# Gates of a product-key expert layer: element-wise adds into a zeroed DRAM array in place of one-hot matrices, on one Trainium2 core

## The chip, the core and the metric

The kernel runs on one core of a Trainium2 chip. The metric is the device time of one execution in microseconds (us); before the change the median of 3 runs is 3128.93 us (3125.25 to 3133.51). A core has TensorE (PE, its weight loads PEld), VectorE (DVE), ScalarE (ACT), GpSimd (POOL) and SyncE (SP); DMAs are issued by SP, ACT and POOL. L12 is line 12 of a kernel; lines of the kernel before and of the changed one differ, and the texts name the kernel where it isn't plain.

## What is computed

512 tokens of 1024 channels and 16 meta tokens pass through two layers. Each has a mixer (pooling in layer 0, stick-breaking attention in layer 1) and then an expert layer, PEER, with 128x128 = 16384 experts. PEER is what the change is about (q, the two halves of the keys and the experts u, v are inputs):

```python
s = einsum('bthpc,hpnc->bthpn', q, sub_keys)              # 8 heads, 2 halves, 128 keys
top_s, top_i = top_k(s, 16)
cand_s = top_s[..., 0, :, None] + top_s[..., 1, None, :]  # 256 candidates
cand_i = top_i[..., 0, :, None] * 128 + top_i[..., 1, None, :]
best_s, best_pos = top_k(cand_s, 16)
expert = take_along_axis(cand_i, best_pos)
gate = softmax(best_s)
act = gelu(einsum('btd,bthkd->bthk', h, u[expert]))
y = einsum('bthk,bthkd->btd', gate * act, v[expert])
```

A token thus has 8 heads x 16 slots = 128 pairs of an expert and a gate. The same expert can come up in several heads, and then its gates add; within one head the 16 experts are distinct.

## The kernel before

Tokens lie in four tiles of 128. Both layers run `peer` (L255). **Tile 3 is gathered** (`GATHERED`): for each of its 128 pairs an indirect DMA from POOL (L343, `row`) fetches one expert's u and v for each of the 128 tokens, 128 rows of 8 KB, and DVE forms the dot product (L355, `prod`) and adds the weighted v (L367, `hx`). Layer 0's meta tokens do the same with 16 more. These gathers are called rows below; `row_step` (L372) issues them a piece at a time, paced by `ROW_PERIOD`, in four buffers (`NROW`).

**Tiles 0 to 2 (384 tokens) are dense:** every block j of 128 experts is computed for every token, whether chosen or not. A u step (L307, matmuls L314) multiplies u of block j with the 384 tokens: fp32 is made of a high and a low part, so each product is three matmuls, 24 of 128x384 in a step, with ACT splitting off the high part (`w_hi`, L279) and DVE or POOL the low part (`w_lo`, L281 and L283). Its gelu, `ac`, goes to DRAM (`aout`). A v step (L660, matmuls L690) reads it back, multiplies it with the block's gates (`wt`, zero where the expert is not chosen) and adds wt times v into six PSUM banks y: 18 matmuls of 128x512.

So the gates have to be spread from 128 pairs to one number for each of 16384 experts and 384 tokens, 25 MB (`gout` in DRAM). Before the change `build_gates` (L553) does it in blocks of four tokens: DVE builds fp16 one-hot matrices of the two key indices by comparing with `iota_x` and multiplies the gate in, as a high and a low fp16 part (L593 to L596); PE multiplies two 128x128 matrices for each token and part (L574, L576, 8 matmuls in a block, 768 in a layer); ACT copies the result to `stage` (L581) and a DMA of 2 MB writes 32 tokens. The v step loads gates of four blocks j as `gt`, in pieces of 512 bytes.

A layer's PEER has three stages. In the **top-16 stage** each head's query is projected (L507, L508 in layer 0, L123 to L125 in layer 1), scored against the keys (L521), and DVE finds the 16 best in each half for each tile (`top16`, L391: MAX8, FIND_INDEX8, MATCH_REPLACE8); for tile 3 `select` (L399) then finds the 16 best pairs and their gates, also by one-hot comparisons (L439, L442, L445). POOL makes the `w_lo` here. A written plan mixes u steps in by estimated costs (`WQ_DVE`, `WQ_PE`). In the **gates stage** `gate_stream` (L606) selects for one dense tile at a time over all heads and then builds its gates; costs yielded by it (`DVE_SLACK`) decide after how much of it a quarter of a u step or a row step follows, and the matmuls' order on PE is pinned to that. In the **v stage** v steps and the remaining u steps run; PE has little else.

Each engine takes its instructions in an order fixed at build time, and a DMA issued by an engine stands in that engine's order.

Of the kernel before, what the change touches and what calls it, by code (L numbers as in the profile page):

```python
# [8 lines left out]
F32 = mybir.dt.float32  # L9
F32R = mybir.dt.float32r  # L10
F16 = mybir.dt.float16
BF = mybir.dt.bfloat16  # L12
I32 = mybir.dt.int32
# [21 lines left out]
GSCALE = 32768.0  # L35
NCAND = 80
TB = 32
FRONT = 3
UPARTS = 4
TG = 4  # L40
GLAG = 2
DVE_SLACK = 1.08
# [15 lines left out]
def trunk_kernel(ctx: ExitStack, tc: tile.TileContext, x, meta, norm_mix, norm_ffn, pool_w, pool_scale,  # L58
# [12 lines left out]
    iota_x = const([P, P, TG], F16, "iota_x")  # L71
# [12 lines left out]
    sy.dma_start(hx[0], x[0, :P, :])  # L84

# [43 lines left out]
    def pool_mixer(gain, normed):  # L129
        with tc.tile_pool(name="pm", bufs=1, reuse_waits="tile") as s1, \  # L130
# [8 lines left out]
            v.tensor_copy(iota_x, iota_f.unsqueeze(2).to_broadcast([P, P, TG]))  # L139
# [101 lines left out]
            pre(0)  # L241
            fold()
            for i in range(1, NT):
                pre(i)
            mixed(NT, hm, None)
            mixed(0, hx[0], NT)
            mixed(1, hx[1], 0)
# [7 lines left out]
    def peer(layer, with_meta, gain, hn_nat, kp, up, finish):  # L255
        gathered = list(GATHERED)
        dense = [i for i in range(NT) if i not in gathered]
        nd = len(dense)
        c0 = dense[0] * P
        assert dense == list(range(dense[0], dense[0] + nd))  # L260
        ND = nd * P
        NB = ND // TB
        gout = dram.tile([P, NB, NK, TB], F32, name=f"gout{layer}")
# [4 lines left out]
        with ExitStack() as cl:  # L268
# [5 lines left out]
            def load_w(src):  # L274
# [12 lines left out]
            pinned = [False]  # L287
            gating = [False]

            def pin(x):  # L290
                return tc.keep_in_program_order(x) if pinned[0] else x

# [14 lines left out]
            def u_parts(j, spill, following=None):  # L307
# [3 lines left out]
                for k in range(KC):  # L311
                    for a, b, st, en in ((whi, hi, k == 0, False), (whi, lo, False, False),
                                         (wlo, hi, False, k == KC - 1)):
                        m = pin(pe.matmul(ps[:, :ND], a[:, k, :], b[:, k, c0:c0 + ND], start=st, stop=en))  # L314
# [11 lines left out]
            def u_step(j, spill, following=None):  # L326
                return drained(u_parts(j, spill, following))

# [8 lines left out]
            def row_steps():  # L337
                flight = []

                def fetch():  # L340
                    item = todo.pop(0)
                    row = gr.tile([P, 2 * D], F32, name="row", bufs=NROW)
                    gp.indirect_dma_start(out=row, out_offset=None, in_=peer_uv,  # L343
                                          in_offset=bass.IndirectOffsetOnAxis(ap=item[1], axis=0))
# [37 lines left out]
            with ExitStack() as c1:  # L382
                tp = c1.enter_context(tc.tile_pool(name="tp", bufs=1, reuse_waits="tile"))
                ps1 = c1.enter_context(tc.tile_pool(name="ps1", bufs=2, reuse_waits="tile", space=PSUM))
                tv = [tp.tile([P, H, 2, TK], F32, name=f"tv{i}") for i in range(NT)]
# [13 lines left out]
                def select(tmp, outp, tag, tvi, tii, nh, res):  # L399
# [3 lines left out]
                    def st(name, dt=F32):  # L403
                        return tmp.tile([P, H * TK], dt, name=name)[:, :ns]
# [648 lines left out]
```

## Time and profile before

| | |
|---|---|
| median of 3 runs | 3128.93 us (3125.25 to 3133.51) |
| profiled execution, its own time | 3127.99 us |
| its span, first to last instruction | 3126.3 us |
| mean granted TensorE clock (1 is 2.4 GHz) | 0.984 |
| busy: PE, DVE, ACT, POOL | 96%, 78%, 43%, 22% |
| DMA | 758.52 MB, mean 243 GB/s |
| PEER of layer 0: top-16, gates, v stage | 55 to 233, 233 to 641, 641 to 1399 us |
| attention | 1399 to 1794 us |
| PEER of layer 1 | 1794 to 1988, 1988 to 2382, 2382 to 3122 us |

Busy shares are time in instructions; since matmuls overlap, their modelled ends make PE look full where one simply follows another, so what one costs is the distance of starts. The chain of what ended last is followed back from the last instruction to what released each step. The table by stage gives busy times in each stretch, the clock and the DMA rate. The stages were bounded by the first and last u, pg and y matmuls of each layer.

### The profile page before, as it was taken

What the parts mean: (1) busy time and instruction counts of PE and PEld (TensorE: products, weight loads), DVE (VectorE), ACT (ScalarE), POOL (GpSimd) and SP (SyncE); (2) the same over time, 40 slices, a digit from 0 to 9 for tenths busy, and PEclk for the clock granted to TensorE, in tenths of its full rate; (3) what the DMA queues carried; (4) which work ended last, traced back from release to release, by engine and by line L of the source; (5) the groups of instructions that cost most, each with busy time, mean ns of one, the idle gap of its engine ahead of it and who ended that gap; (6) DMA issues with size and microseconds to landing.
All of it is one profiled execution on the core that took longest, in us unless ns stands there. A gap on an engine that the chain in (4) does not pass through costs nothing.

```text
span 3126.3 us, 45813 instructions
## 1 busy us (share of the span) xinstructions
PE 2999.0 (96%) x16514; PEld 2671.7 (85%) x16514; DVE 2449.1 (78%) x5636; ACT 1354.3 (43%) x2184; POOL 688.7 (22%) x704
## 2 busy tenths in 40 slices
PE   8988999999999999999999989799999999999999
PEld 7887988988888888879965778798898888888887
DVE  3999998878777778786456469999987777777765
ACT  3443645643333333335455334354655333333333
POOL 3431311111111111114245244222110111111100
PEclk9999999999999999999999999999999999999999
DMA  3435877799989899762100344477878998989875
GB/s 134 179 121 202 282 265 265 274 360 329 338 312 321 314 329 329 273 245 90 55 1 1 108 177 144 158 262 269 303 253 326 358 314 321 331 308 333 307 250 164
DMA packets 286708, 758.52 MB, mean 243 GB/s; under 512 B 23184, under 2 KB 176784, under 8 KB 248336
## 3 DMA queue, kind: packets, MB, share of 16 engines
q1 hardware_dynamic: 222544, 390.92, 36.8%
q0 software_dynamic: 39168, 285.23, 24.9%
q10 hardware_dynamic: 24768, 79.44, 6.6%
q8 instruction: 129, 2.11, 0.3%
q14 instruction: 99, 0.81, 0.1%
HBM read 673.99 MB, written 81.53 MB: 242 GB/s over the span
## 4 chain that ended last, share of the span: by engine, by line
PE 77%; DVE 16%; DMA 3%; ACT 2%; issue 1%; POOL 0%; SPq 0%; DVEq 0%; ACTq 0%; POOLq 0%
PE y L690 31%; PE psu L314 27%; PE pg L574 3%; PE pg L576 3%; PE pp L124 2%; PE pp L125 2%; PE pp L123 2%; DVE mr L395 1%; DVE prod L355 1%; DVE w_lo L281 1%; DMA gt<-gout 1%; DVE ti L397 1%; DVE hx L367 1%; DMA w<-in_peer_ut_dram 1%; DVE ti L394 1%
## 5 line engine op out<-in xcount | busy, mean ns | idle before, releaser
L343 POOL DMA_INDIRECT row<-in_peer_uv_dram,ei x272 | 383.3, 1409 | 1833.1 <-DVE hx L367 1481.9
L314 PE MATMUL psu<-n_hi,w_lo 128*128 128x384 f32 x2048 | 701.5, 343 | 42.4 <-DVE w_lo L281 39.9
L314 PE MATMUL psu<-n_hi,w_hi 128*128 128x384 f32 x2048 | 720.4, 352 | 11.5 <-ACT ac L321 7.2
L314 PE MATMUL psu<-n_lo,w_hi 128*128 128x384 f32 x2048 | 703.0, 343 | 0.6 <-DVE n_lo L118 0.6
L279 ACT ACTIVATE w_hi<-w 128x1024 fp32r<-128x1024 f32 x288 | 305.6, 1062 | 467.7 <-PE psu L314 373.2
L690 PE MATMUL y<-v_lo,wt_hi 128*128 128x512 f32 x1536 | 473.6, 390 | 1.6 <-DVE v_lo L676 1.6
L690 PE MATMUL y<-v_hi,wt_hi 128*128 128x512 f32 x1536 | 473.8, 390 | 0.5 <-ACT v_hi L675 0.5
L690 PE MATMUL y<-v_hi,wt_lo 128*128 128x512 f32 x1536 | 473.6, 389 | 0.0
L314 PEld LDWEIGHTS psu<-n_hi,w_lo 128*128 128x128 f32 x2048 | 394.0, 192 | 49.0 <-DVE w_lo L281 45.8
L314 PEld LDWEIGHTS psu<-n_hi,w_hi 128*128 128x128 f32 x2048 | 395.4, 193 | 17.8 <-ACT ac L321 7.5
L314 PEld LDWEIGHTS psu<-n_lo,w_hi 128*128 128x128 f32 x2048 | 394.0, 192 | 5.5 <-DVE n_lo L118 1.1
L682 ACT ACTIVATE wt_hi<-wt 128x384 fp32r<-128x384 f32 x256 | 134.3, 525 | 574.0 <-PE y L690 295.5
L683 DVE TENSOR_TENSOR wt_lo<-wt,wt_hi 128x384 fp32r<-128x384 f32 x256 | 142.5, 557 | 264.3 <-ACT wt_hi L682 264.3
L281 DVE TENSOR_TENSOR w_lo<-w,w_hi 128x1024 fp32r<-128x1024 f32 x228 | 278.2, 1221 | 83.2 <-ACT w_hi L279 82.6
L690 PEld LDWEIGHTS y<-v_lo,wt_hi 128*128 128x128 f32 x1536 | 288.1, 188 | 63.3 <-DVE v_lo L676 2.9
L690 PEld LDWEIGHTS y<-v_hi,wt_lo 128*128 128x128 f32 x1536 | 288.3, 188 | 60.4
L355 DVE SCALAR_TENSOR_TENSOR prod<-row,hnat 128x1024 bf16<-128x1024 f32 x272 | 337.7, 1241 | 0.6 <-DMA row<-in_peer_uv_dram,ei 0.5
L367 DVE SCALAR_TENSOR_TENSOR hx<-row,gwt,hx 128x1024 f32<-128x1024 f32 x256 | 334.5, 1307 | 2.1
L690 PEld LDWEIGHTS y<-v_hi,wt_hi 128*128 128x128 f32 x1536 | 286.8, 188 | 52.8 <-ACT v_hi L675 0.9
L676 DVE TENSOR_TENSOR v_lo<-v,v_hi 128x1024 fp32r<-128x1024 f32 x256 | 312.2, 1219 | 5.4 <-ACT v_hi L675 5.2
L581 ACT ACTIVATE stage<-pg 128x512 f32<-128x512 f32 x192 | 216.9, 1137 | 149.2 <-PE pg L576 146.3
L675 ACT ACTIVATE v_hi<-v 128x1024 fp32r<-128x1024 f32 x256 | 270.8, 1058 | 10.6 <-DMA v<-in_peer_uv_dram 9.5
(313 smaller groups left out, 4695.0 us busy)
## 6 DMA issues: line engine op xcount, KB each, us to landing
w<-in_peer_ut_dram SPq DMA_DIRECT2D x256, 512.0 KB, 5.9
v<-in_peer_uv_dram SPq DMA_DIRECT2D x256, 512.0 KB, 6.1
gout<-stage ACTq DMA_DIRECT2D x24, 2048.0 KB, 8.4
gt<-gout SPq DMA_DIRECT2D x64, 768.0 KB, 10.2
aout<-ac ACTq DMA_DIRECT2D x148, 192.0 KB, 4.0
ac<-aout SPq DMA_DIRECT2D x148, 192.0 KB, 5.9
w<-in_peer_wq_dram SPq DMA_DIRECT2D x32, 512.0 KB, 3.4
wn<-in_w_kv_dram SPq DMA_DIRECT2D x8, 1024.0 KB, 5.5
```

Source lines behind the costliest of these rows:

```text
L279: amark.append(sc.activation(whi, w, AF.Copy))
L281: vmark.append(v.tensor_sub(wlo, w, whi.bitcast(F32)))
L314: m = pin(pe.matmul(ps[:, :ND], a[:, k, :], b[:, k, c0:c0 + ND], start=st, stop=en))
L343: gp.indirect_dma_start(out=row, out_offset=None, in_=peer_uv, in_offset=bass.IndirectOffsetOnAxis(ap=item[1], axis=0))
L355: v.scalar_tensor_tensor(prod, row[:, :D], 1.0, hn_nat[i], ALU.mult, ALU.mult, accum_out=dot)
L367: v.scalar_tensor_tensor(acc, row[:, D:], wt, acc, ALU.mult, ALU.add)
L581: sc.activation(stage[:, :, o:o + TG].rearrange("p j t -> p t j"), pg, AF.Copy, scale=1.0 / GSCALE)
L675: amark.append(sc.activation(vhi, v32, AF.Copy))
L676: vmark.append(v.tensor_sub(vlo, v32, vhi.bitcast(F32)))
L682: sc.activation(whi, wt, AF.Copy)
L683: vmark.append(v.tensor_sub(wlo, wt, whi.bitcast(F32)))
L690: pe.matmul(y[n][half], wp[:, ts], vq[:, half * 512:(half + 1) * 512], start=st, stop=en)
```

## The change

The gates of the dense tiles are no longer built but added into place. `gout` is an array of 6,291,456 floats for each layer, laid out as key 1, key 2, token. It is zeroed ahead of time (`clear_gates`): in layer 0 by six DMAs of 4.2 MB that ACT issues during the pooling mixer, in layer 1 by four during the attention. In the top-16 stage `select` now runs once per head, over all four tiles (64 slots a token), and `gates_out` computes with two DVE operations an address `at` for each pair. `scatter` then issues, from POOL, one indirect DMA with an add for each head, tile and slot: 128 addresses, one for each partition, 4 bytes each. There are 8x3x16 = 384 in a layer; 27 are issued in each head's place in the program, the rest between the u steps that follow, up to the 122nd (`EARLY`). As adds of different heads may meet at one element, a head's scatters wait for those of the head before on the same tile. The gate matrices, their matmuls, stage copies and 2 MB writes go, and the gates stage with its pinned order: after the top-16 stage there are u steps, with row steps at a new `ROW_PERIOD`, then the v stage. All `w_lo` are made by DVE. `gt` becomes [128, 4, 384] with 6 KB in one run, and its load waits for the last head's scatters.

```diff
-ROW_PERIOD = ((18.0, 13.5), (18.0, 13.5))
-WQ_DVE = (19.0, 19.0)
-WQ_PE = (15.5, 12.5)
+ROW_PERIOD = (12.0, 13.0)
+WQ_DVE = 27.5
+WQ_PE = (15.5, 14.5)
-QUIET = 16
+EARLY = 122
+SCATTER_A = 27
...
+    gouts = [dram.tile([P * NK * ND, 1], F32, name=f"gout{layer}") for layer in range(2)]
+    cleared = [[], []]
+    def clear_gates(layer, part, parts):
+        g = gouts[layer].rearrange("(p c f) o -> p c (f o)", p=P, f=512)
+        n = NK * ND // 512 // parts
+        cleared[layer].append(sc.dma_start(g[:, part * n:(part + 1) * n, :],
+                                           zero.unsqueeze(1).to_broadcast([P, n, 512])))
...
-                if gating[0]:
-                    vmark.append(v.tensor_sub(wlo, w, whi.bitcast(F32)))
-                else:
-                    gp.tensor_sub(wlo, w, whi.bitcast(F32))
+                vmark.append(v.tensor_sub(wlo, w, whi.bitcast(F32)))
...
+            def gates_out(h, i1, i2, gate):
+                ef = gr.tile([P, nd, TK], F32, name="gf", bufs=2)
+                at = gr.tile([P, nd * TK], I32, name=f"at{h}")
+                ds = slice(0, nd * TK)
+                v.scalar_tensor_tensor(ef, i1[:, ds].rearrange("p (n q) -> p n q", q=TK), float(ND),
+                                       tok[:, :nd].unsqueeze(2).to_broadcast([P, nd, TK]), ALU.mult, ALU.add)
+                v.scalar_tensor_tensor(at, i2[:, ds], float(NK * ND), ef.rearrange("p n q -> p (n q)"),
+                                       ALU.mult, ALU.add)
+                to_scatter.extend((h, n, at[:, n * TK + q:n * TK + q + 1], gate[:, n * TK + q:n * TK + q + 1])
+                                  for n in range(nd) for q in range(TK))
+            def scatter(count):
+                for _ in range(min(count, len(to_scatter))):
+                    h, n, at, gate = to_scatter.pop(0)
+                    x = gp.indirect_dma_start(out=gout, out_offset=bass.IndirectOffsetOnAxis(ap=at, axis=0),
+                                              in_=gate, in_offset=None, compute_op=ALU.add)
+                    if issued:
+                        after(x, issued[0], sync=False)
+                    issued.append(x)
+                    earlier = placed[n, h - 1] if h else cleared[layer]
+                    for e in earlier:
+                        after(x, e)
...
                 def fetch():
...
+                    for y in issued:
+                        after(x, y, sync=False)
+                    issued[:] = [x]
...
+                        i1, i2, gate = select(qp, gr, f"h{h}", tv, ti, NT)
+                        gates_out(h, i1, i2, gate)
+                        scatter(SCATTER_A)
                         for i in gathered:
-                            res = []
-                            for _ in select(qp, gr, f"g{i}_{h}", tv[i][:, h:h + 1], ti[i][:, h:h + 1], 1, res):
-                                pass
-                            gather_rows(i, h, *res, TK, hx[i], False)
-                        while tr < tq and row_step():
-                            tr += ROW_PERIOD[layer][0] / 8
+                            of = slice(i * TK, (i + 1) * TK)
+                            gather_rows(i, h, i1[:, of], i2[:, of], gate[:, of], TK, hx[i], False)
...
+                left = len(to_scatter)
+                first = j0
                 tu = tr = 0.0
+                while j0 < EARLY:
+                    u_step(j0, True, ("u", j0 + 1))
+                    j0 += 1
+                    scatter(left * (j0 - first) // (EARLY - first) - (left - len(to_scatter)))
+                    tu += ucost
+                    while tr < tu and row_step():
+                        tr += ROW_PERIOD[layer] / 8
+                scatter(len(to_scatter))
...
+                        gts[jg] = vp.tile([P, JG, ND], F32, name="gt", bufs=3)
+                        x = sy.dma_start(gts[jg], gates[:, jg * JG:(jg + 1) * JG, :])
+                        for n in range(nd):
+                            for e in placed[n, H - 1]:
+                                after(x, e)
```

What the change does to the order, at the places that the prediction speaks of.

POOL in layer 0's top-16 stage, before (`row` is a gather of tile 3, `ei_0` the expert numbers of head 0, `w_lo` a low part; "x3" is three in a row):

```order
L283 TENSOR_TENSOR w_lo<-w_1183,w_hi 128x1024
L343 DMA row<-in_peer_uv_dram,ei_0_988 128x2048 x3
L283 TENSOR_TENSOR w_lo<-w_1217,w_hi 128x1024
L343 DMA row<-in_peer_uv_dram,ei_0_988 128x2048
L283 TENSOR_TENSOR w_lo<-w_1323,w_hi 128x1024
L343 DMA row<-in_peer_uv_dram,ei_0_988 128x2048
```

and with the change (`at_1008` are the addresses of head 0, `h0gate` its gates):

```order
L353 DMA gout_82<-h0gate,at_1008 6291456x1 x48
L353 DMA gout_82<-h1gate,at_1538 6291456x1 x48
L353 DMA gout_82<-h2gate,at_1932 6291456x1 x48
L353 DMA gout_82<-h3gate,at_2326 6291456x1 x48
L353 DMA gout_82<-h4gate,at_2720 6291456x1 x25
L380 DMA row<-in_peer_uv_dram,ei_0_1040 128x2048 x3
L353 DMA gout_82<-h4gate,at_2720 6291456x1 x4
L380 DMA row<-in_peer_uv_dram,ei_0_1040 128x2048
L353 DMA gout_82<-h4gate,at_2720 6291456x1 x2
L380 DMA row<-in_peer_uv_dram,ei_0_1040 128x2048
```

The w_lo are gone from POOL, and 217 scatters stand ahead of the first gather, where there was none. Gathers follow among the remaining scatters. The waits of the first of them (a name with DMASW is one of eight semaphores that POOL's DMAs use in turn):

```order
L353 DMA gout_82<-h0gate,at_1008 6291456x1 x7
L353 DMA gout_82<-h0gate,at_1008 6291456x1 [waits DMASW0_49]
L353 DMA gout_82<-h0gate,at_1008 6291456x1 [waits DMASW1_49]
L353 DMA gout_82<-h0gate,at_1008 6291456x1 [waits DMASW2_49]
```

From the ninth on each waits for the DMA that used its semaphore before, eight places ahead.

DVE at the end of layer 0's top-16 stage, with the change (the last head's selection ends some ten rows above; `tvm`, `tim` and this `cand` belong to the meta tokens, `prod` to the first gather):

```order
L434 MAX tvm<-mr_3961 128x8
L447 TENSOR_TENSOR cand_3967<-tvm 128x16
L289 TENSOR_TENSOR w_lo<-w_4069,w_hi 128x1024
L435 MAX_INDEX tim<-tvm,mr_3961 128x8
L447 TENSOR_TENSOR cand_3967<-tvm 128x32
L395 SCALAR_TENSOR_TENSOR prod,dot<-row,hnat_92 128x1024
L431 MAX bv<-cand_3967 128x8
L472 CAST tib_4002<-tim 128x32
L289 TENSOR_TENSOR w_lo<-w_4113,w_hi 128x1024
```

The first product that needs a row stands behind the last head's selection, one split ahead of it and the others behind it; before, products stood among the searches of every head.

By the same orders of PE, 24.2 u steps precede layer 0's last score (9.1 before) and 26.25 precede layer 1's (14.25 before); 38 and 40 w_lo stand on DVE between the first search and the end of the top-16 stage. 66.9 and 65.8 u steps stood in the gates stages. With the change 63 rows of layer 0 stand ahead of the last scatter on POOL and 81 behind it, and 57 and 71 in layer 1; 126 u steps precede the first v step. On ACT the first clear stands ahead of its first ACTIVATE.

## Rows read from the trace of the kernel before

**Rows 1.** The page, chain that ended last: shares of the span by engine and by line.

```profile
PE 77%; DVE 16%; DMA 3%; ACT 2%; issue 1%; POOL 0%; SPq 0%; DVEq 0%; ACTq 0%; POOLq 0%
PE y L690 31%; PE psu L314 27%; PE pg L574 3%; PE pg L576 3%; PE pp L124 2%; PE pp L125 2%; PE pp L123 2%; DVE mr L395 1%; DVE prod L355 1%; DVE w_lo L281 1%; DMA gt<-gout 1%; DVE ti L397 1%; DVE hx L367 1%; DMA w<-in_peer_ut_dram 1%; DVE ti L394 1%
```

**Rows 2.** By stage: us, PE, PEld, DVE, ACT, POOL busy (x), PEclk, DMA share, GB/s.

```profile
55.00:233.00 178.00, 157.01 (x1127) 152.69 (x1125) 152.85 (x757) 73.02 (x133) 71.58 (x38) 0.95 0.42 147
233.00:641.00 408.00, 379.64 (x2345) 358.40 (x2344) 372.47 (x1017) 215.83 (x278) 80.98 (x33) 0.97 0.72 258
641.00:1399.00 758.00, 756.35 (x3622) 664.52 (x3623) 600.40 (x864) 288.48 (x474) 115.98 (x105) 1.00 0.89 317
1399.00:1794.00 395.00, 380.32 (x2498) 307.84 (x2496) 216.44 (x448) 189.82 (x437) 145.25 (x276) 0.98 0.17 54
1794.00:1988.00 194.00, 173.34 (x863) 152.15 (x864) 160.20 (x759) 78.19 (x110) 86.17 (x43) 0.96 0.43 152
1988.00:2382.00 394.00, 368.90 (x2287) 348.79 (x2285) 360.62 (x954) 210.13 (x271) 69.39 (x32) 0.97 0.73 262
2382.00:3122.00 740.00, 739.03 (x3526) 647.43 (x3526) 561.25 (x800) 277.56 (x446) 97.72 (x86) 1.00 0.86 303
```

**Rows 3.** Chain in the v stage of layer 0: start, us, what.

```profile
712.30 4.23 PE psu L314 x24
716.53 8.18 PE y L690 x36
```

**Rows 4.** Timeline of PE in the gates stage: start, us, instruction.

```profile
331.07 0.29 PE L574 MATMUL pg<-ab 128*128 128x128 f16 x1
...
331.54 0.30 PE L574 MATMUL pg<-ab 128*128 128x128 f16 x1
```

**Rows 5.** Timeline of PE, start of layer 0's top-16 stage.

```profile
55.48 0.44 PE L314 MATMUL psu<-n_hi,w_hi 128*128 128x384 f32 x1 [0.25 <-ACT n_hi L117]
...
77.39 0.61 PE L521 MATMUL ps<-keys,qt 128*128 128x128 f32 x4
```

**Rows 6.** Timeline of DVE: searches over 128 and over 80 candidates.

```profile
219.45 0.28 DVE L393 MAX8 tv<-s 128x8 f32<-128x128 f32 x1
...
220.62 0.28 DVE L393 MAX8 tv<-s 128x8 f32<-128x128 f32 x1
...
272.05 0.23 DVE L393 MAX8 bv<-cand 128x8 f32<-128x80 f32 x1
...
272.97 0.23 DVE L393 MAX8 bv<-cand 128x8 f32<-128x80 f32 x1
```

**Rows 7.** Groups of DVE by form, 55 to 650 us: count, busy, mean ns, idle before.

```profile
L281 DVE TENSOR_TENSOR w_lo<-w,w_hi 128x1024 fp32r<-128x1024 f32 x65 | 79.1, 1217 | 21.2 <-ACT w_hi L279 21.2
...
L445 DVE TENSOR_REDUCE gdi<-oh 128x128 f32<-128x2048 bf16 x6 | 13.7, 2278 | 0.0
...
L442 DVE TENSOR_TENSOR oh<-oh,tib 128x2048 bf16<-128x2048 bf16 x6 | 7.3, 1217 | 0.0
...
L439 DVE TENSOR_TENSOR oh<-iota_b,da 128x2048 bf16<-128x2048 bf16 x3 | 6.8, 2280 | 0.0
...
L424 DVE SCALAR_TENSOR_TENSOR da<-sh 128x16 f32<-128x16 uint32 x9 | 1.5, 172 | 0.2
```

**Rows 8.** Gathers: by line in 55:260, 260:645, 645:1400; all, min/median/max ns; landing.

```profile
L343 POOL DMA_INDIRECT row<-in_peer_uv_dram,ei x13 | 15.5, 1189 | 56.9 <-DVE gwt L363 28.2 <-DVE oh L442 17.9 <-DVE tv L393 5.7
...
L343 POOL DMA_INDIRECT row<-in_peer_uv_dram,ei x30 | 76.3, 2543 | 301.7 <-DVE hx L367 259.9 <-DVE du L431 13.9 <-DVE du L432 10.7
...
L343 POOL DMA_INDIRECT row<-in_peer_uv_dram,ei x101 | 114.5, 1133 | 613.1 <-DVE hx L367 483.5 <-DVE gain L367 76.2 <-DVE gwt L363 42.6
...
L343 POOL DMA_INDIRECT row<-in_peer_uv_dram,ei x272: 937/1011/6507, 98.6 to 2990.8; - x136
...
DMA to landing us min/median/max: 5.4/8.6/15.6
```

**Rows 9.** By stretch of 20 us, as rows 2: inside layer 0's v stage.

```profile
700.00:720.00 20.00, 20.00 (x100) 17.96 (x99) 17.89 (x25) 7.52 (x13) 3.90 (x4) 1.00 1.01 402
```

More of the change, by code (lines that the diff above doesn't have):

```diff
@@ L84, in trunk_kernel @@
     sy.dma_start(hx[0], x[0, :P, :])
+    dense = [i for i in range(NT) if i not in GATHERED]
+    nd = len(dense)
+    assert dense == list(range(nd))
+    ND = nd * P
+    gouts = [dram.tile([P * NK * ND, 1], F32, name=f"gout{layer}") for layer in range(2)]
[5 more added lines that the diff above has]
+                                           zero.unsqueeze(1).to_broadcast([P, n, 512])))
     n_hi = const([P, KC, S + NM], F32R, "n_hi")
@@ L256, in peer @@
         gathered = list(GATHERED)
[L257 to L263, printed above, removed]
+        gout = gouts[layer]
         aout = [dram.tile([P, ND], F32, name=f"aout{layer}_{j}") for j in range(NK)]
@@ L313, in u_parts @@
                                          (wlo, hi, False, k == KC - 1)):
-                        m = pin(pe.matmul(ps[:, :ND], a[:, k, :], b[:, k, c0:c0 + ND], start=st, stop=en))
+                        m = pe.matmul(ps[:, :ND], a[:, k, :], b[:, k, :ND], start=st, stop=en)
                         n += 1
@@ L327, in u_step, with after @@
                 return drained(u_parts(j, spill, following))
+            to_scatter = []
+            placed = {}
+            issued = []
+            def gates_out(h, i1, i2, gate):
[8 more added lines that the diff above has]
+                                  for n in range(nd) for q in range(TK))
+            def after(x, y, sync=True):
+                kind = mybir.DependencyClass.Sync if sync else mybir.DependencyClass.NoSync
+                tc.add_manual_dep(x.ins, y.ins.name, mybir.DependencyInfo(kind, mybir.DependencyReason.DATA),
+                                  reason="gates")
+            def scatter(count):
[9 more added lines that the diff above has]
+                        after(x, e)
+                    tc.declare_no_dep(x.ins, group=f"gates{layer}", keep=[e.ins for e in earlier],
+                                      reason="one head's slots of a token are distinct experts")
+                    tc.add_to_no_dep_group(f"gates{layer}", x.ins)
+                    placed.setdefault((n, h), []).append(x)
             def gather_rows(i, h, i1, i2, gate, ns, acc, first):
@@ L479, in peer @@
                         plan += [("w", 2 * h), ("w", 2 * h + 1)]
-                        td += WQ_DVE[layer]
+                        td += WQ_DVE
                         tu += WQ_PE[layer]
@@ L645, in peer @@
                 gts = {}
+                gates = gout.rearrange("(p j t) o -> p j (t o)", p=P, j=NK)
                 order = []
@@ L864, in attention @@
                 with tc.issue_after(last.ins):
+                    for part in range(4):
+                        clear_gates(1, part, 4)
                     tables = sc.preload_act_table_set("natural_log_exp_and_others")
```

141 lines of the change are left out of this document (25 added, 116 removed).

## Prediction

> **What bounds the kernel now.** I read the chain that ended last first: 77% of it is PE and 16% DVE; its two largest parts are the y matmuls (L690) and the psu matmuls (L314), and the gate matmuls L574 and L576 have 3% each [rows 1]. So a microsecond counts where it shortens PE's work or fills a hole in it. The table by stage says where the holes are [rows 2]; its first three rows are layer 0's PEER (top-16 stage, gates stage, v stage), the last three layer 1's, and the row between them is the attention. Layer 0 takes 178+408+758 = 1344 us, with 21+28+2 = 51 us in which PE is idle; at granted clocks of 0.95 and 0.97 the first two stages also lose about 5% and 3% of their length, 9+12 = 21. Layer 1 takes 194+394+740 = 1328, idle 21+25+1 = 47, clock loss 8+12 = 20. In the v stages PE has no hole and the clock is 1.00, while the DMA engines are 86 to 89% busy: a second limit, close by. One u step there is 4.23 us, two v steps 8.18 [rows 3].
>
> **What is removed.** Of the 1536 gate matmuls, 768 in a layer, four start in 0.47 us (331.07 to 331.54) [rows 4]: 90 us of PE per layer. DVE's one-hot operations of L593 to L596, ACT's stage copies and 24 transfers of 2 MB go as well; in the v stages, where PE is full, they are long over, so they are worth what the gates stage gains from it: it no longer holds its 67 u steps against DVE, and its idle time and clock loss go. PE's bare work is then 1344-90-51-21 = 1182 us in layer 0 and 1328-90-47-20 = 1171 in layer 1.
>
> **The new top-16 stage.** The selection of all tiles moves into it, head by head, on DVE. One head: eight top-16 searches over 128 (219.45 to 220.62: 1.17 each, 9.4), four over 80 candidates (0.92 each, 3.7) [rows 6]; two halves of one-hot selection at 1024 elements, together like one half at 2048 (2.28+1.22+2.28 = 5.8); some 28 small operations of 0.17 (4.8) [rows 7]. Sum 23.7. All w_lo splits that POOL did are now DVE's: 38 in layer 0's stage and 40 in layer 1's, 1.22 us each less the 0.08 by which neighbours overlap, 43 and 46 us. The first score comes 22 us after the first u matmul [rows 5]; 23 with its copy. So DVE needs 23+8x23.7+43 = 256 us (layer 1: 259). PE's work there: before, 157 busy less 9 of clock is 148; 24.2 u steps instead of 9.1 add 15.1x4.23 = 64: 212. Layer 1: 173-8+12x4.23 = 216. DVE is the bound; PE idles **44** and **43** us.
>
> **The scatters.** POOL's order is the new risk. 217 scatters stand ahead of the first row gather; the first of DVE's products that needs a row stands right after the last head's selection, and two w_lo splits later nothing can pass it. POOL starts when head 0's selection is done, 23+23.7 and four splits, 51 us into the stage. With s us per scatter the last of the 217 is out at 51+217s, and the row lands 8.6 us after its issue (the median). DVE comes to it at 256. DVE's stall is 217s-196 us (layer 1: 217s-199). PE has some 6 us of split weights in hand, 1.4 u steps.
> Neither a scatter nor an accumulating DMA is in this trace. Nearest rows: POOL's row gathers, which also address 128 places each. They take POOL 1.13 us on average in the v stage, 1.19 in the top-16 stage and 2.54 in the gates stage (median of all 1.01, least 0.94) [rows 8]. Below, s is 0.94. Above, 2.54; and as a POOL DMA waits for the one eight before it, landings of 5.4, 8.6 and 15.6 us would make s at least 0.68, 1.08 and 1.95. I take **1.05**, close to the least, the median and the top-16 stage, whose DVE work is the same kind: the long gathers lie among the fp16 one-hot operations, which are gone. That stall is 32-6 = **26** and 29-6 = **23** us.
> The v stage's DVE does little but splits and products of two inputs, and its gathers average 1.13: such neighbours alone don't make a gather long [rows 8]. The Trainium skill ("GPSIMD Engine Reference", section 8, Key points) speaks against this choice: GpSimd shares its SBUF interfaces with VectorE, with contention beside DVE instructions that have two SBUF inputs. By it the new splits in the stage would lengthen scatters and the sum would be that of rival 3; by the row it stays at 1.05.
> The other 167 scatters go between u steps, 1.7 per step beside 0.64 rows: 1.7x1.05+0.64 = 2.4 us of POOL per 4.23, covered. The cover is gone at s = 2.1.
>
> **The rest.** The v stage starts when the last scatter has landed; the first gt load waits on SP's queue and holds back the loads behind it, for about one landing. I allow 10 us in layer 0 and 5 in layer 1 for this and for the traffic: with 81 rows behind the last scatter in some 550 us, a v step of layer 0 (4.09 us) asks for 0.92 MB (v, spilled activations, gates) and 0.63 MB of rows, 379 GB/s, where the trace has held 402 over 20 us with PE full but 317 over the v stage [rows 2, 9]; a u step asks for 0.72 MB and 0.67 MB of rows, 329 GB/s. The gt loads themselves become 128 runs of 6 KB instead of pieces of 512 bytes, worth nothing while PE hides them. The clears, 25 MB each, are free in layer 1 (the attention moves 54 GB/s) but in layer 0 stand on ACT's queue ahead of its first work and share the engines with the first loads: 0 to 25 us, taken as **10**.
>
> **Sum.** Layer 0: 1182+44+26+10+10 = 1272, 72 less than 1344. Layer 1: 1171+43+23+5 = 1242, 86 less. The profiled execution took 3127.99 us with a span of 3126.3; it becomes 3128-158 = **2970**. It lies 1 us below the median of the runs, so the forecast for the median is the same.
>
> **Rivals.**
> 1. *Scatters are too slow, and the kernel becomes slower.* POOL's queue is the one place: the gain of 158 is eaten when 2x217x(s-1.05) reaches it, at s = 1.41, a landing of 11.3 us on eight lanes. At the longest landing of a gather, s = 1.95: 195 us more stall per layer, and 2.34 DMAs x1.95 = 4.6 us per u step against 4.23, 32 more over 98 steps: 2970+454 = about 3425. For it: such landings and long gathers exist. Against: 512 bytes per scatter where a row has a megabyte. Chance 0.17.
>    If scatters went one after another at twice a gather's issue, s = 2.0, 206 us more stall per layer would make it about 3380; the gathers speak against it, since they are issued well within one landing of 8.6 us of each other, and I give that variant 0.03 of the 0.17. The Trainium skill ("DMA: Bandwidth & Descriptors", Anatomy of one DMA) states such a price, about 2.0 us of fixed time for a DMA from GpSimd, most of it the write's receipt; no run here shows it for a scatter.
> 2. *DMA becomes the bound.* If no more than 330 GB/s comes through (the v stages have 303 and 317), a v step of layer 0 takes 1.55/330 = 4.70 us instead of 4.09 and one of layer 1, with 71 rows, 4.46; 126 steps give 77+47, less the 15 already allowed: 2970+109 = about 3080; at 325 with the u steps 3110. For: DMA engines busy for 86 to 89%. Against: the 512-byte pieces that help to fill them go. Chance 0.18.
> 3. *DVE's splits lengthen scatters.* The splits are a fifth of the stage; if a scatter beside one takes the gates stage's 2.54, s is 0.8x1.0+0.2x2.54 = 1.3, 217x0.25 = 54 us more per layer: about 3080. For: the gates stage. Against: the v stage. Chance 0.05.
> 4. *The backlog is free.* At s = 0.94 DVE's stall is 8 and 5, within PE's 6 us; nothing slips at the gt loads and the clears: 2970-49-25 = about 2895. Chance 0.1.
> 5. *The change doesn't do what it says.* If the top-16 stages swallowed what PE saves (it would take 10 us more per head, as waits between DVE and ACT at every selection would), the time stays within 3120 to 3138. Nothing in the trace shows waits of that size. Chance 0.03.
>
> **Numbers.** The forecast, 2970, has 0.47. The range reaches from just below the fourth rival to the upper end of the second, 2880 to 3110, and leaves out the first and the fifth. About 0.3%, 9 us, can be told from no change: faster 0.8, same 0.03, slower 0.17.
>
> **What would show it.** Right: PE loses the 180 us of gate matmuls and its holes lie in the top-16 stages alone, the granted clock is 1.00 outside the top-16 stages, the stages' ends are 256 to 290 us after the first u step, and DVE waits there once per layer for a row. POOL's scatters start every 1.0 to 1.1 us. Wrong: scatters over 1.4 us apart, PE waiting for w_lo while DVE waits for a row for over 100 us; or PE waiting for v or w in the v stage at over 340 GB/s; or a long hole in front of the first y matmul, from gt.

## The result and the profile after

The changed kernel takes 3535.4 us (median of 4 runs, 3519.17 to 3546.86) against 3128.6 before: a ratio of 1.1295, 95% interval 1.1248 to 1.1342. It is 13% slower; the forecast was 2970 and its range ended at 3110. Of the cases named ahead it is the first rival, scatters that are too slow, whose price had been given as about 3425. The signs that the prediction had named for it came as well: scatters over 1.4 us apart, and PE waiting for a w_lo while DVE waits for a row for over 100 us.

The page of the changed kernel, its busy line and the two lines of the chain that ended last:

```profile
PE 2858.3 (81%) x14960; PEld 2541.5 (72%) x14960; DVE 2202.0 (62%) x4773; ACT 1138.8 (32%) x1962; POOL 1812.3 (51%) x1414
...
PE 39%; POOL 24%; DVE 12%; DMA 12%; issue 10%; ACT 2%; ACTq 1%; SPq 0%; DVEq 0%; POOLq 0%
POOL gout L353 22%; PE y L650 21%; PE psu L314 7%; DMA v<-in_peer_uv_dram 5%; DMA row<-in_peer_uv_dram,ei 4%; POOL row L380 2%; PE pp L135 2%; PE pp L136 2%; PE pp L134 2%; DVE w_lo L289 2%; DVE v_lo L637 1%; ACTq L94 1%; DVE prod L395 1%; DVE mr L433 1%; DMA gout<-h5gate,at 1%
```

PE had 77% of the chain [rows 1]; now the scatters (L353) alone have 22%, more than the y matmuls. PE lost the gate matmuls, and its busy share fell from 96% to 81% of a longer span.

The table by stage of the changed kernel, cut at the ends of PE's holes (columns as in rows 2: us, PE, PEld, DVE, ACT and POOL busy with counts, PEclk, DMA share, GB/s). Rows two to five are layer 0's PEER, row six the attention, the last four layer 1's PEER:

```profile
0.00:92.00 92.00, 46.19 (x256) 41.02 (x256) 25.71 (x45) 21.70 (x38) 16.47 (x91) 0.98 0.96 354
92.00:373.00 281.00, 254.58 (x1655) 248.14 (x1656) 239.88 (x1101) 106.03 (x170) 197.25 (x118) 0.95 0.49 108
373.00:572.00 199.00, 0.72 (x5) 0.40 (x3) 2.55 (x5) 1.25 (x3) 166.08 (x109) 0.51 0.25 12
572.00:1059.00 487.00, 432.63 (x2302) 423.45 (x2303) 288.70 (x400) 153.21 (x263) 396.03 (x231) 0.94 0.94 293
1059.00:1602.00 543.00, 536.75 (x2354) 440.40 (x2353) 466.05 (x694) 210.06 (x338) 88.23 (x80) 1.00 0.93 352
1602.00:2046.00 444.00, 384.45 (x2499) 311.92 (x2497) 224.40 (x451) 190.37 (x437) 140.02 (x274) 0.93 0.30 105
2046.00:2327.00 281.00, 251.68 (x1285) 226.40 (x1285) 237.13 (x1080) 105.79 (x140) 194.44 (x118) 0.96 0.51 109
2327.00:2524.00 197.00, 1.51 (x8) 1.18 (x7) 3.94 (x8) 1.53 (x3) 164.41 (x108) 0.51 0.26 15
2524.00:2994.00 470.00, 416.06 (x2252) 408.09 (x2252) 265.50 (x335) 145.97 (x248) 381.33 (x225) 0.95 0.93 286
2994.00:3535.00 541.00, 533.74 (x2356) 440.48 (x2354) 448.10 (x660) 202.88 (x325) 68.09 (x66) 1.00 0.90 338
```

The profiled execution's span grew by 409 us, from 3126.3 to 3535.4; where, can be read off against rows 2. Layer 0's PEER begins at 92 instead of 55 us (+37) and takes 1510 instead of 1344 (+166); the attention takes 444 instead of 395 (+49); layer 1's PEER 1489 instead of 1328, of which the last 4 us lie behind its last matmul as before (+157). In the third and the eighth row PE, DVE and ACT do next to nothing for almost 200 us and only POOL works. These two stretches are called the holes below. The granted clock there is 0.51, the lower of its two levels, with PE idle; in the u steps behind it is 0.94.

What ended those waits, in the waits of the whole kernel (us in total, times, longest):

```profile
DVE prod L395 <- DMA row<-in_peer_uv_dram,ei: 597.8, 70, 201.9
PEld psu L314 <- DVE w_lo L289: 539.2, 63, 198.7
PE psu L314 <- DVE w_lo L289: 520.2, 56, 198.4
```

DVE stands for 201.9 us at the first product, for a row; the w_lo splits behind it on DVE are late, and PE stands for 198.4 us for a w_lo. And why the row is late, in POOL's timeline at its first scatters:

```profile
143.57 1.78 POOL L353 DMA_INDIRECT gout<-h0gate,at  x1 [48.80 <-DVE tv L434]
145.66 1.57 POOL L353 DMA_INDIRECT gout<-h0gate,at  x1 [0.30 <-issue]
147.53 1.56 POOL L353 DMA_INDIRECT gout<-h0gate,at  x1 [0.30 <-issue]
149.39 1.56 POOL L353 DMA_INDIRECT gout<-h0gate,at  x1 [0.30 <-issue]
```

One scatter takes POOL 1.56 us, and 0.30 more pass before the next. POOL waits there for nothing else. By stretch, from the first to the last scatter of layer 0 and of layer 1:

```profile
143.00:1029.00 886.00, 621.95 (x3534) 607.86 (x3534) 476.61 (x1324) 231.32 (x382) 749.16 (x448) 0.85 0.69 181
2098.00:2965.00 867.00, 605.03 (x3214) 577.85 (x3214) 453.88 (x1243) 224.89 (x348) 732.36 (x442) 0.86 0.69 178
```

POOL's 448 DMAs of layer 0 are busy for 749 us, and 448 x 0.30 is 134: 883 of the 886 us. From its first scatter to its last POOL has no slack: its queue is the bound of the kernel until the v stage may begin.

### The profile page after: what moved, and what is told of

Read it like the earlier page. It is cut to its first block, busy times and chain, and to the rows that moved or that the text cites. A ratio compares the mean times of both kernels' runs of the same rounds, so it can differ in the third digit from the quotient of the medians.

```text
span 3535.4 us, 42744 instructions
## 1 busy us (share of the span) xinstructions
PE 2858.3 (81%) x14960; PEld 2541.5 (72%) x14960; DVE 2202.0 (62%) x4773; ACT 1138.8 (32%) x1962; POOL 1812.3 (51%) x1414
## 4 chain that ended last, share of the span: by engine, by line
PE 39%; POOL 24%; DVE 12%; DMA 12%; issue 10%; ACT 2%; ACTq 1%; SPq 0%; DVEq 0%; POOLq 0%
POOL gout L353 22%; PE y L650 21%; PE psu L314 7%; DMA v<-in_peer_uv_dram 5%; DMA row<-in_peer_uv_dram,ei 4%; POOL row L380 2%; PE pp L135 2%; PE pp L136 2%; PE pp L134 2%; DVE w_lo L289 2%; DVE v_lo L637 1%; ACTq L94 1%; DVE prod L395 1%; DVE mr L433 1%; DMA gout<-h5gate,at 1%
## 5 line engine op out<-in xcount | busy, mean ns | idle before, releaser
L314 PE MATMUL psu<-n_hi,w_lo 128*128 128x384 f32 x2048 | 718.4, 351 | 520.4 <-DVE w_lo L289 520.2
L314 PEld LDWEIGHTS psu<-n_hi,w_lo 128*128 128x128 f32 x2048 | 402.8, 197 | 539.7 <-DVE w_lo L289 539.2
L380 POOL DMA_INDIRECT row<-in_peer_uv_dram,ei x272 | 324.3, 1192 | 864.6 <-DVE hx L407 752.2
L314 PE MATMUL psu<-n_lo,w_hi 128*128 128x384 f32 x2048 | 714.9, 349 | 0.6 <-DVE n_lo L129 0.6
L289 DVE TENSOR_TENSOR w_lo<-w,w_hi 128x1024 fp32r<-128x1024 f32 x288 | 352.0, 1222 | 191.5 <-ACT w_hi L288 172.8
L399 ACT ACTIVATE ga<-dot 128x1 f32<-128x1 f32 x272 | 53.9, 198 | 862.1 <-DVE prod L395 850.8
L353 POOL DMA_INDIRECT gout<-h0gate,at x96 | 159.7, 1664 | 127.5 <-DVE tv L434 98.9
```

The source lines that it names most:

```text
L314: m = pe.matmul(ps[:, :ND], a[:, k, :], b[:, k, :ND], start=st, stop=en)
L353: x = gp.indirect_dma_start(out=gout, out_offset=bass.IndirectOffsetOnAxis(ap=at, axis=0), in_=gate, in_offset=None, compute_op=ALU.add)
L380: x = gp.indirect_dma_start(out=row, out_offset=None, in_=peer_uv, in_offset=bass.IndirectOffsetOnAxis(ap=item[1], axis=0))
```

## The experiments

Theory A: POOL's queue. A scatter costs POOL nearly 2 us, and all that stands behind it in order waits. Rivals: scatters complete slowly and hold each other; their traffic holds the rest; only the order is at fault.

**What makes one scatter long.** Probes at the start of the changed kernel, on POOL:

```diff
+    for k in range(8):
+        gp.indirect_dma_start(out=pr[1][k], out_offset=on0, in_=zero[:, :1], in_offset=None, compute_op=ALU.add)
+    for k in range(8, 16):
+        gp.indirect_dma_start(out=pr[1][k], out_offset=on0, in_=zero[:, :1], in_offset=None)
+    for k in range(16, 24):
+        gp.indirect_dma_start(out=pr[1][k], out_offset=half, in_=zero[:64, :1], in_offset=None, compute_op=ALU.add)
+    for k in range(8):
+        gp.indirect_dma_start(out=got[:, k:k + 1], out_offset=None, in_=pr[1][k], in_offset=on0)
+    for k in range(8):
+        gp.indirect_dma_start(out=pr[512][k], out_offset=on0, in_=zero, in_offset=None)
+    for k in range(8, 16):
+        gp.indirect_dma_start(out=pr[512][k], out_offset=on0, in_=zero, in_offset=None, compute_op=ALU.add)
```

> The changed kernel with 48 indirect DMAs more on POOL at its start, eight of each of six kinds, into small arrays of their own: an add of one float per partition, the same without the add, the add on 64 partitions, a gather of one float, a write of 512 floats per partition, and the same with an add. What counts is how long POOL takes for one of each, not the time of the kernel. The scatters of the changed kernel took 1.55 us and then 0.30 us until the next, a gather of a row 0.94 to 1.0. Theory A, the add makes the issue long: about 1.55 us with an add of either size, about 1.0 without. Theory B, the small element does: 1.55 for both kinds of one float and for the gather of one float, 1.0 for 512 floats. Theory C, the write to DRAM does: 1.55 for all writes, 1.0 for the gather. The add on 64 partitions: 0.8 if the issue goes by addresses, 1.5 if it goes by DMA.

Groups of POOL in this kernel (count, busy us, mean ns, idle before). L108 is the add of one float, L110 the write of one float, L112 the add on 64 partitions, L114 the gather of one float, L116 the write and L118 the add of 512 floats:

```profile
L108 POOL DMA_INDIRECT pr<-zero,idx x8 | 12.6, 1570 | 58.4 <-DMA pr<-zero 57.8 <-issue 0.6
L118 POOL DMA_INDIRECT pr<-zero,idx x8 | 12.5, 1560 | 2.4 <-issue 2.4
L112 POOL DMA_INDIRECT pr<-zero,idx x8 | 11.4, 1424 | 40.8 <-DMA pr<-zero,idx 30.7 <-DMA pr<-zero 9.5 <-issue 0.6
L116 POOL DMA_INDIRECT pr<-zero,idx x8 | 7.7, 964 | 2.4 <-issue 2.4
L110 POOL DMA_INDIRECT pr<-zero,idx x8 | 7.7, 964 | 33.9 <-DMA pr<-zero,idx 16.3 <-DMA pr<-zero 16.1 <-issue 1.5
L114 POOL DMA_INDIRECT got<-pr,idx x8 | 7.6, 955 | 16.7 <-DMA pr<-zero,idx 15.8 <-issue 0.9
```

The add is the cause: 1.56 to 1.57 us with it, 0.96 without, whether 4 bytes or 2 KB go per address and whichever way they go. Half the addresses save 0.15 us only, so the price is one of the DMA more than of its addresses. The 0.30 us between two stand before every one (the eight of L116 and of L118 each have 2.4 us of idle). The kernel as a whole took 3741.13 us in its one run, since the probes stand ahead of the mixer's work on POOL: the first u matmul starts at 291 instead of 92 us.

**No scatters at all.**

```diff
                     h, n, at, gate = to_scatter.pop(0)
+                    placed.setdefault((n, h), [])
+                    continue
```

> The changed kernel without its 768 scatters (the dense tiles' gates stay zero); the clears, the selection and the address operations stay. Theory A, the scatters' time on POOL's queue is what the kernel lost: the two holes of 199 and 197 us of PE behind the top-16 stages go, and the u steps behind them shrink from 487 and 470 us to about 425: 3535-199-197-62-55 = about 3020, and still 37 and 45 us late through the clears. Rival, the traffic: rows and weights wait for DMA engines that the scatters don't fill: the holes shrink by less than half, over 3250.

Measured: 3005.0 us, 0.9601 of before (0.9567 to 0.9636), theory A's 3020 and not the rival's 3250. By stage, layer 0's top-16 stage, u steps and v stage:

```profile
92.00:373.00 281.00, 255.14 (x1660) 248.71 (x1661) 244.40 (x1118) 106.18 (x172) 7.05 (x8) 0.95 0.38 124
373.00:788.00 415.00, 408.66 (x2301) 407.36 (x2300) 285.62 (x386) 153.89 (x264) 78.32 (x65) 0.99 0.93 338
788.00:1328.00 540.00, 535.23 (x2355) 439.72 (x2354) 465.44 (x695) 209.87 (x338) 85.77 (x80) 1.00 0.93 354
```

The hole is gone and the u steps take 415 us instead of 487; the top-16 stage and the v stage are what they were. The scatters cost all of 530 us; without them, and so without the dense tiles' gates, the kernel is 4% faster than before.

**Three quarters of them.**

```diff
-                                  for n in range(nd) for q in range(TK))
+                                  for n in range(nd) for q in range(TK) if q % 4 != 3)
-SCATTER_A = 27
+SCATTER_A = 20
```

> The changed kernel with 12 of each head's 16 slots scattered (every fourth slot of the dense tiles is left out), 20 instead of 27 in a head's place: 161 scatters ahead of the first gather instead of 217, 127 instead of 167 behind it. Theory A, DVE's wait is the POOL queue's length times 1.93 us (1.55 to 1.7 of issue, 0.30 to the next, as the changed kernel's top-16 stage shows): the holes of 199 and 197 us shrink by 56x1.93 = 108 to about 91 and 89, the u steps behind them from 487 and 470 us to 430 to 440, together 3535-2x(108+45) = about 3230. Rival, what holds the rows is that scatters complete slowly or wait for one head after the other: the holes shrink by less than 60 us and the kernel stays over 3350.

Measured: 3194.14 us, 1.0197 (1.0152 to 1.0243), 36 us under theory A's 3230 and far from the rival's 3350. Layer 0's top-16 stage, hole and u steps:

```profile
93.00:373.00 280.00, 253.53 (x1660) 246.84 (x1658) 239.89 (x1102) 106.54 (x170) 196.37 (x116) 0.95 0.49 108
373.00:470.00 97.00, 0.77 (x5) 0.45 (x3) 2.10 (x5) 0.83 (x2) 80.85 (x54) 0.52 0.26 20
470.00:890.00 420.00, 411.37 (x2304) 410.35 (x2305) 290.34 (x399) 153.85 (x265) 318.73 (x192) 0.99 1.02 341
```

The hole is 97 us where 91 was expected, the u steps 420. 56 scatters fewer take 102 us off it, 1.8 us each: the hole follows the length of POOL's queue. Scatters that waited for one another's ends would shrink it too, with their number; against that speaks the changed kernel's own trace, in which the end of a DMA released POOL 16 times in 768 scatters, for 4.8 us in all, 0.3 each as between any two.

**Rows between the scatters.**

```diff
+                        while tr < 29.4 * (h + 1) and row_step():
+                            tr += ROW_A / 8
-SCATTER_A = 27
+SCATTER_A = 14
+ROW_A = 18.0
```

> The changed kernel with gathers put between the scatters already in the top-16 stage (14 scatters and some three rows for each head instead of 27 and none), all 768 scatters kept. Theory A1, POOL's sum of work sets the start of the v stage, whatever the order: the holes of 199 us shrink to under 40, but the v stage can't start before 51 us + 384 scatters x 1.93 + some 90 rows x 1.3 = 910 us from the stage's start instead of 967: about 3535-2x57 = 3420, the u steps taking the wait. Theory A2, only the order is at fault, the scatters hide behind u steps when the rows don't stand behind them: about 3535-2x(197+60) = 3020.

Measured: 3721.82 us, 1.1882 (1.1848 to 1.1917): slower than the changed kernel, and both expectations missed. From layer 0's first scatter to its last:

```profile
146.00:1126.00 980.00, 689.01 (x3558) 663.08 (x3558) 541.15 (x1431) 236.60 (x412) 780.36 (x475) 0.84 0.69 194
```

The long hole is gone, but POOL needs 980 us instead of 886 from its first scatter to its last: 780 busy, 475 x 0.30 = 143 between, and 57 in which it waits, mostly at gathers, for DVE, with scatters behind. Two rows of its waits in that stretch (us in total, times, longest):

```profile
POOL row L381 <- DVE hx L408: 33.3, 7, 10.6
POOL row L381 <- DVE gwt L404: 20.1, 7, 5.1
```

The 94 us more, twice, are the 186 us by which it is slower. The sum on POOL's queue sets the start of the v stage in this order too, as A1 has it, but later than A1 had reckoned: 1055 us after the stage's start instead of 910 (967 in the changed kernel). A1's sum held 858 us of POOL from the first scatter to the last where 980 were measured: scatters took 2.04 us instead of 1.93 from one to the next, gathers 1.54 instead of 1.3, and the 57 us of waits were not in it. A2 missed by 700 us. Without the holes there are 281+415-51 = 645 us from POOL's start to the v stage, and 384 scatters at 1.86 are 714: by these numbers no order would have hidden them all.

**Writes instead of adds.**

```diff
-                                              in_=gate, in_offset=None, compute_op=ALU.add)
+                                              in_=gate, in_offset=None)
```

> The changed kernel with the scatters writing instead of adding (where two heads choose the same expert for a token, one gate is lost). If the add makes a scatter's issue long, s falls from 1.86 us to about 1.3 and the holes from 199 us to 217x1.3-196 = 86, the u steps behind them to about 430: 3535-2x113-115 = about 3195. If the small element or the write to DRAM does, s stays at 1.86 and the kernel within 20 us of 3535.

Measured: 3488.88 us, 1.1148 (1.1111 to 1.1184). A miss of both expectations. POOL's part came as the probes have it: a scatter takes 0.96 us (the median), 1.26 to the next. But layer 0's top-16 stage with its hole takes 508 us, 281+199 in the changed kernel:

```profile
92.00:600.00 508.00, 282.54 (x1606) 265.03 (x1606) 234.15 (x1065) 102.33 (x165) 225.80 (x230) 0.73 0.22 66
```

and every engine waits in it again and again, as in these rows of its waits ("issue" and "remote": for nothing that the profile shows):

```profile
ACT w_hi L288 <- remote: 237.1, 8, 50.1
PEld psq L542 <- issue: 84.6, 41, 10.8
PE psq L542 <- issue: 81.1, 39, 10.5
DVE w_lo L289 <- remote: 59.6, 2, 53.4
```

With the selection late, POOL had to wait for it, 96 us in all. What holds the engines beside plain 4-byte writes is open. So this run doesn't show in the kernel what the probes show alone, except in the u steps behind: they take 438 us instead of 487 with the shorter scatter.

**Clears away from ACT.** Layer 1's four clears, issued by SP behind the last w_kv load:

```diff
-                        clear_gates(1, part, 4)
+                        x = clear_gates(1, part, 4, sy)
+                        tc.add_manual_dep(x.ins, last.ins.name, mybir.DependencyInfo(
+                            mybir.DependencyClass.Sync, mybir.DependencyReason.DATA), reason="late")
```

> The changed kernel with layer 1's four clears issued by SP, after the last w_kv load, instead of by ACT ahead of its table load; layer 0's stay. Theory A, ACT's queue is held for 42.7 us while it issues them: the attention falls from 444 us to 395 to 402 and the kernel to 3535-45 = about 3490. Rival, the clears' traffic delays the attention whoever issues them: it stays within 10 us of 3535.

Measured: 3483.32 us, 1.113 (1.1098 to 1.1162), 52 us less than the changed kernel; the attention takes 403 us instead of 444. Most of the other 11 us lie in layer 0, where the two kernels are the same; runs of the changed kernel differ by up to 28. In the changed kernel's timeline of ACT this is what went:

```profile
1787.76 42.72 ACTq L94 DMA_DIRECT2D gout<-zero  x4
1830.51 1.28 ACT L827 ACT_TABLE_LOAD   x1 [42.37 <-issue]
```

ACT's queue is held for 42.7 us while it issues four transfers of 6 MB, and the attention's exponentials stand behind. The same four transfers hold SP's queue for 43.6 us in this run, but SP has nothing else to do there, and the attention is within 8 us of its 395 before the change.

**A version that beats both.** By the prediction's sum for the hole (the end of POOL's queue less DVE's arrival) 113 scatters ahead of the first row are free, and 127 behind it were nearly so in the run with three quarters of them. So tile 2's gates go back to one-hot matrices, in the u steps:

```diff
+    ns = nd - 1
+    NS = ns * P
-    gouts = [dram.tile([P * NK * ND, 1], F32, name=f"gout{layer}") for layer in range(2)]
+    gouts = [dram.tile([P * NK * NS, 1], F32, name=f"gout{layer}") for layer in range(2)]
...
+                building = build_gates(*hots)
...
+                    if (j0 - first) % HOT_EVERY == 0:
+                        next(building, None)
...
-                    v.tensor_mul(wt, ac, gts[jg][:, j % JG, :])
+                    v.tensor_mul(wt[:, :NS], ac[:, :NS], gts[jg][:, j % JG, :])
+                    v.tensor_mul(wt[:, NS:].rearrange("p (b t) -> p b t", t=TB), ac[:, NS:].rearrange("p (b t) -> p b t", t=TB),
+                                 hts[jg][:, :, j % JG, :])
-SCATTER_A = 27
+SCATTER_A = 14
```

> A mixture: tiles 0 and 1 get their gates by scatters as in the changed kernel, tile 2 by one-hot matrices as before (32 blocks in a layer, one after every second u step), 14 scatters in a head's place, layer 1's clears on SP as in the run e2, the arrays two thirds as large. 256 scatters in a layer instead of 384, 113 ahead of the first gather. Theory A: DVE's wait is 113x1.93-220 = none, the other 143 hide behind u steps as the 127 of the run e4 did; PE pays 256 gate matmuls a layer, 30 us. From the 3005 us of the run without scatters: -45 for the clears, +60 for the matmuls, some 10 less for the smaller clears of layer 0: about 3010, faster than both kernels. Rival: DVE, with one-hot blocks beside splits and row products in the u steps (about 3.6 of 4.2 us), becomes the bound there, or the traffic of stages and scatters does: 3060 to 3130.

Measured: 3056.77 us, 0.9754 (0.9737 to 0.977), 2.5% faster than before. By stage, layer 0's top-16 stage and its u steps up to the first y matmul:

```profile
80.00:360.00 280.00, 256.11 (x1690) 249.24 (x1689) 240.93 (x1111) 109.23 (x176) 191.18 (x113) 0.96 0.48 105
360.00:837.00 477.00, 449.74 (x2580) 440.53 (x2581) 336.31 (x554) 185.42 (x299) 365.70 (x217) 0.97 0.98 323
```

No hole. The time is 47 us above theory A and just under the rival's 3060 to 3130. The u steps take 62 us more than the 415 of the run without scatters, where 30 had been put for the gate matmuls, and layer 1's 57 more (467 instead of 410). PE is idle for 27 of the 477 us instead of 6, waiting 17 us for w_lo and 10 for ac. DVE, the rival's first reason, is busy for 336 of 477 us; the DMA engines, its second, for 0.98 of the time (0.93 without scatters). That the traffic makes the w_lo and ac late fits these numbers but isn't shown.

With two of layer 0's four clears moved behind the first u step, and 12 scatters in a head's place:

```diff
-                clear_gates(0, i, 4)
+                if i == 1:
+                    clear_gates(0, i, 4)
...
+                    for part in (2, 3) if layer == 0 else ():
+                        x = clear_gates(0, part, 4, sy)
```

> The mixture of the run e6, but of layer 0's four clears only the first two stay on ACT in the pooling mixer; the other two go to SP behind the first u step's matmuls, and 12 instead of 14 scatters stand in a head's place (97 ahead of the first gather). If the clears' traffic and their place on ACT's queue delay the mixer (0.82 of the DMA engines in the first 80 us of e6), layer 0's first u matmul comes some 15 to 25 us earlier than at 88 us and the kernel takes about 3040. Rival: the same bytes then hold up the weights of the first heads or the first scatter, which waits for the last clear, and the gain is given back: 3050 to 3065.

Measured: 3053.92 us, 0.9749 (0.9733 to 0.9765), no different from the run before, and in the rival's range. In the execution that was profiled the first u matmul came at 77 instead of 88 us, and the first y matmul at 828 instead of 838; that execution is also the fastest, 3042.96 us, where the other three took 3052.81 to 3056.85. So the median shows no gain, and whether the 11 us are kept is open. No run leaves out layer 0's clears altogether.

## Why the prediction was wrong

- **What bounds the kernel, and what is removed: right.** The run without scatters is the forecast less its scatter terms: 2970-26-23 = 2921 us, and with what the clears cost over the forecast, 27 in layer 0 and 49 in the attention, 2997; measured 3005. PE's bare work and the freed 90 us per layer hold. DVE came to the end of its selection after 275 us, not 256, but that cost little: PE had u steps to fill the time with. In the run without scatters PE is idle for 26 of the 281 us, and at a granted clock of 0.95 loses some 14 more, where 44 had been forecast.
- **The step that failed: "I take 1.05" for a scatter's s.** The runs showed 1.94 on average ahead of the first gather (217 scatters from 143.6 to 563.7 us): 0.96 for an indirect DMA, 0.60 for the add, 0.30 between two, and 0.08 on average for some that take up to 2.5 us. The 0.30 could have been read: the gathers [rows 8] were taken by their duration, while matmuls [rows 4] and searches [rows 6] were taken from start to start. POOL's timeline of the kernel before has it at its first gathers:

```profile
98.64 1.19 POOL L343 DMA_INDIRECT row<-in_peer_uv_dram,ei  x1 [2.98 <-DVE tv L393]
100.14 0.94 POOL L343 DMA_INDIRECT row<-in_peer_uv_dram,ei  x1 [0.30 <-issue]
101.38 0.94 POOL L343 DMA_INDIRECT row<-in_peer_uv_dram,ei  x1 [0.30 <-issue]
```

  With 1.25 for s the sum would have had about 87 us more. The 0.60 of the add could not be read; no row had an add.
- **The law was right.** The stall was put at the queue's end, 51+217s, plus a landing of 8.6 us, less DVE's arrival. With s = 1.94 that is 481, and with DVE's arrival at 275, 206 us. In the changed kernel's timeline of DVE it is 202, as the first row landed 5.7 us after its issue:

```profile
569.45 1.25 DVE L395 SCALAR_TENSOR_TENSOR prod<-row,hnat 128x1024 bf16<-128x1024 f32 x1 [201.92 <-DMA row<-in_peer_uv_dram,ei]
```

  PE's holes are 199 and 197. The point at which the gain is eaten, s = 1.41, stands by the probes' numbers between plain writes (1.26) and adds (1.86).
- **"Covered" u steps: wrong.** The other 167 scatters and 63 gathers were put at 2.4 us per u step. Among the u steps a scatter was busy for 1.86 us on average and a gather for 1.35, with 0.30 behind each: 1.7x2.16+0.64x1.65 = 4.7 us of 4.23. The steps took 487 and 470 us, 72 and 60 more than without scatters; rival 1 had put this at 32 us a layer.
- **Neighbours on DVE: rival 3's mechanism came.** It has DVE's splits lengthen scatters, by the rule of the Trainium skill ("GPSIMD Engine Reference", section 8), and the prediction set it aside. The trace agrees with the rule. POOL's timeline in the top-16 stage, and what DVE runs on two tensors at that time:

```profile
227.89 1.92 POOL L353 DMA_INDIRECT gout<-h0gate,at  x1 [0.30 <-issue]
230.11 2.03 POOL L353 DMA_INDIRECT gout<-h0gate,at  x1 [0.30 <-issue]
232.45 1.55 POOL L353 DMA_INDIRECT gout<-h0gate,at  x1 [0.30 <-issue]
...
227.16 1.22 DVE L289 TENSOR_TENSOR w_lo<-w,w_hi 128x1024 fp32r<-128x1024 f32 x1
228.50 1.21 DVE L289 TENSOR_TENSOR w_lo<-w,w_hi 128x1024 fp32r<-128x1024 f32 x1
229.90 0.68 DVE L447 TENSOR_TENSOR cand<-tv 128x128 f32<-128x128 f32 x4
```

  The third scatter has searches beside it and takes 1.55 us. Laid side by side in this way, layer 0's 177 scatters without any TENSOR_TENSOR or SCALAR_TENSOR_TENSOR of DVE beside them take 1.55 us on average and never over 1.8, in the hole and among u steps with the DMA engines at 0.95 alike; the 105 among u steps with 0.7 us or more of these beside them take 2.01. So it is the neighbour that goes with the length, not the traffic. Ahead of the first gather this adds 0.08 to s, the smallest part of the 0.89 by which s was missed. Among the u steps it adds 0.30: at 1.86 from one scatter to the next and 1.3 for a gather POOL would have needed 4.0 us per u step, and the cover would have held. The prediction's reason against it was the v stage's average of 1.13 [rows 8]; but there too the 8 of 101 gathers with no such neighbour take 0.94 us, and the 78 with 0.7 us or more of them 1.19. In the gates stage, with its 2.54, the 23 of 30 with 0.7 us or more take 3.03 us and the other 7 take 0.94.
- **Layer 1's clears: "free", measured 49 us in the attention,** of which 41 went when SP issued them. That the DMA engines have room [rows 2] was true; the queue that issues them was left out of the sum, though it had been named for layer 0. **Layer 0's clears: 10 of a range of 0 to 25, measured 37.** Both things that the prediction named are in the chain and in ACT's timeline: the load of `pscale`, which DVE had waited 0.3 us for before, lands 19.7 us after its issue, with the DMA engines at 0.96, and behind it the clears hold ACT's queue, the last three for 33 us:

```profile
3.32 19.65 DMA pscale<-in_pool_scale_dram
...
30.95 13.85 ACTq L94 DMA_DIRECT2D gout<-zero  x1
44.90 10.70 ACTq L94 DMA_DIRECT2D gout<-zero  x1
57.98 8.27 ACTq L94 DMA_DIRECT2D gout<-zero  x1
```

- **The v stage: right.** 128 v steps of 4.09 us are 523; with two late u steps and 10 or 5 of allowance, 541 and 536; measured 543 and 541 with the tail. Rival 2 did not come: 352 GB/s went through with PE full.
- **The Trainium skill's price** ("DMA: Bandwidth & Descriptors", Anatomy of one DMA) of some 2.0 us for a DMA from GpSimd came close to the s that was measured, but not by its reason: the page puts most of it on the write's receipt, and here POOL itself is busy for 1.56 us, and waits for completions come to 4.8 us in 768 scatters.

## What to carry to other kernels

Price an instruction in a queue by the distance of starts in a run of its kind, not by its duration, and add up a whole queue from the first instruction to the last that something waits for: 384 DMAs at even 1.25 us are 480 us of POOL in a layer. An indirect DMA that adds kept POOL busy 1.6 times as long as one that writes, and for 64 addresses almost as long as for 128. So its number has to fit under the work at hand, and what needs other DMAs of the same queue must not stand behind more of them than fit; here two tiles of three did. When one engine's instructions vary in length, lay its timeline beside its neighbours': an average over a stage hid what DVE does to POOL's DMAs. A large transfer that is cheap for the DMA engines can still hold the engine that issues it: 25 MB issued from ACT's queue took 42.7 us of ACT.

## What the runs showed of the hardware

In the probes the add raises POOL's time for an indirect DMA of 128 addresses from 0.96 to 1.56 us, with 4 bytes per address and with 2 KB; 64 addresses take 1.42. Beside DVE's instructions on two tensors (0.7 us or more of them) a scatter among the u steps takes 2.01 us on average, without them 1.55. In the hole, up to the first gather, the scatters' DMA keeps the 16 engines 0.23 busy while they move 0 GB/s as rounded: 190.7 x 0.23 over 103 scatters is 0.43 us of all 16 engines for 512 bytes. Four clears of 6 MB held the issuing queue for 42.7 us on ACT and 43.6 on SP. Beside plain 4-byte writes at 1.26 us apart the whole core slowed in the top-16 stage, with waits that the profile gives no cause for, as it did not beside adds; why is open.
